# A two-layer hybrid decoder step on one core: the first output rows put into other tile places, two groups of side work recorded later, and new estimates for small matmuls

## The chip, the cores and the metric

One core of one Trainium2 chip runs one program. The metric is device time in microseconds (us), the median of the runs; lower is better. The kernel before has three runs: 3142.32, 3144.25 and 3147.87 us.

## The reference, cut to what matters

The program is one inference step of a decoder trunk of two layers over 2064 prompt tokens (16 learned ones ahead of 2048) and 8 samples of one token each. All inputs are 32-bit floats.

```
u = x @ w_in                                  # 1024 -> 5128 channels
A: 512 ch: causal conv, RG-LRU: r, i = sigmoid(xb @ w_a + b_a), sigmoid(xb @ w_x + b_x)
   log_a = -8 r softplus(-lam);  h = scan(exp(log_a), sqrt(1 - exp(2 log_a)) * i * x);  y = h * silu(z)
B: 4 heads of 128: rotary retention in chunks of 64, group norm, * silu(z)
C: 4 heads of 128: conv on q, k, v; gated delta rule in chunks of 64 (triangular solve), rms norm, * silu(z)
mix = concat(y_A, y_B, y_C)                   # 1536 channels
y = layernorm(alpha * x + mix @ w_out) * ln_w + ln_b
```

Beside y the step returns the new states of A, B and C and the last inputs of the convs, for the prompt and for the samples.

## The kernel before

**How the work is tiled.** A layer (`layer`, L551) goes through its tokens in two halves (`sblock`, L594; 1040 tokens, then 1024 with the 8 samples behind them). A half has 16 stages, listed in `STAGES` (L29): K (the keys of a delta head), A (128 channels of the RG-LRU), B (a retention head), C (a delta head). A stage projects its slabs of 128 output channels: 24 matmuls for each slab and block of tokens, since each 32-bit operand is split into a high and a low part and three products are formed over eight slabs of k. The work that follows a projection (gates, scan, retention, delta rule) is a generator that the `Pump` (L282) advances between the matmuls of the next stage's projection. The second half ends with the stages C3, B3, A3. What a branch gives is multiplied by its gate and stored to DRAM by `put_mix` (L660), on POOL's queue (`mix_d<-g`).

**The output stage** (from L1460) takes rows of 128 tokens, 17 of them. For a row, `o_load` (L1476) fetches the mixed channels (`ma`, 8 slabs; `mb`, 4 slabs) and the residual `xr`; `o_split` (L1499) casts them to high parts `ah`, `bh` on ACT and subtracts to low parts `al`, `bh[:, 1]` on DVE; then 2 x 36 matmuls of 512 columns run over the slabs of the output weights in `WO_ORDER` (L1632). Row 0's load is recorded with the last slab of A3 (`last_slab`, L1426), and the load of row r + 1 when row r starts. The output weights come in by `wo_load` (L1634): 12 slabs, each cast on ACT and subtracted on DVE or POOL; ten of them go into the `arena` as the projection has done with a part of the tokens (`wo_free`, L1664). Beside rows 0 and 1 run the ends of B3 and A3: `rglru_gates` (L1362: matmuls `pgt`, activations `r` and `ix`), `rglru_scan` (L1389), the norm of B3 (`pno`, `sn`) and the samples' retention (`samples_ret`, L1178: it loads a state `sv` on POOL's queue and makes `ps` from `swork` and `sv`).

**What sets the order.** All instructions are recorded first (`Recorder`, L62 to L259; its helper is the only line, L268, that the trace shows, so that the rows are told apart by their tiles). `cost` (L160) estimates each duration, and `order` (L190) schedules greedily: the operation that can start earliest, and of those the one recorded first. `places` (L84) adds the waits for tile places: a tag with `bufs` places is handed out in turn, and a new tile in a place waits for the last use of the old one.

**Tile places of the first rows.** Tag "g" has two places, held by B3's and A3's gates while the output stage begins. Row 0's `ah` is the next tile of that tag and takes B3's place; row 1's `ah` takes A3's, which is free when A3's `put_mix` has stored it. `bh` goes by row to "t21" (even) and "cc" (odd), row 0's `xr` to "ap", all other `xr` to "kT".

**The two other pieces.** At the start of a layer DVE computes `hba` (half the gates' biases) and `sp4` (from `softplus`, L411), which only `rglru_gates` and `rglru_scan` read, and POOL's queue copies the older two inputs of the samples' conv from one DRAM tensor to another (`out_cs<-in_convb`, 128 KB).

Of the kernel before, what the change touches and what calls it, by code (L numbers as in the profile page):

```python
# [8 lines left out]
F32 = mybir.dt.float32  # L9
F32R = mybir.dt.float32r  # L10
BF = mybir.dt.bfloat16
AF = mybir.ActivationFunctionType
OP = mybir.AluOpType
# [28 lines left out]
_V = {}  # L42
# [7 lines left out]

class Op:

    __slots__ = ("eng", "name", "emit", "cost", "succ", "left", "ready", "nbytes", "func", "port", "first", "frees", "start", "end")

    def __init__(self, eng, name, emit):
        self.eng, self.name, self.emit = eng, name, emit
        self.succ, self.left, self.ready, self.nbytes, self.func, self.port, self.first, self.frees = [], 0, 0.0, 0, None, False, 1, []


class Recorder:  # L60
# [4 lines left out]


    SETS = {"Exp": 0, "Tanh": 0, "Sqrt": 1}
    SLACK = {"PE": 0.2, "DVE": 0.07, "ACT": 0.07, "POOL": 0.1, "SP": 0.05}

    def __init__(self, tc):  # L70
# [89 lines left out]
    def cost(self, op, out, ins, kw):  # L160
        n, eng = out.free_size(), op.eng
        if eng == "PE":
            m = ins[0].free_size()
            if op.name == "transpose":
                return 0.107 * max(m, out.free_size()) / 128 + 0.002
            if ins[0].dtype == F32:
                return 2 * (max(n, m, 24) / 1200 + 0.004)
            return max(n, 64) / 2400 + 0.0135
        if op.name == "dma_start":
            op.nbytes = out.nbytes() if callable(out.nbytes) else out.nbytes  # L170
            return 0.06 if eng == "SP" else 0.55
        n = max([n] + [x.free_size() for x in ins if x.free_size() <= 2048])
        if eng == "ACT":
            return 0.165 + 0.00083 * n + 0.09 * (len(ins) > 1) + 0.19 * ("accum_out" in kw)
        if eng == "POOL":
            op.port = op.name == "tensor_tensor"
            return 0.1 + n * {"tensor_tensor": 0.00225, "memset": 0.00083}.get(op.name, 0.0011)
        near = [x for x in ins if "PSUM" not in str(x.space)]
        op.port = (sum(x.free_size() >= 8 for x in near) > 1
                   or op.name in ("tensor_scalar", "tensor_copy") and "PSUM" not in str(out.space) and bool(near))  # L180
        if op.name == "tensor_tensor_scan":
            return 0.22 + 0.00208 * n
        step = max((abs(x.ap[-1][0]) for x in ins if len(x.ap) > 1), default=1)
        return 0.15 + 0.00104 * n * (2 if step > 1 else 1) + 0.05 * (len(ins) > 2)
# [5 lines left out]
    def order(self):  # L190
        t = dict.fromkeys(("PE", "DVE", "ACT", "POOL", "SP"), 0.0)
        wait = {e: [] for e in t}
        here = {e: [] for e in t}
        pool, dma, func, out = 0.0, 0.0, None, []
        for i, op in enumerate(self.ops):
            if not op.left:
                heapq.heappush(wait[op.eng], (0.0, i))
        while True:
            best = None
            for e in t:  # L200
                w, h = wait[e], here[e]
                while w and w[0][0] <= t[e]:
                    self.move(w, h)
                s = t[e] if h else w[0][0] if w else None
                if s is not None and (best is None or s < best[0]):
                    best = s, e
            if best is None:
                break
            start, e = best
            t[e] = max(t[e], start)  # L210
            while wait[e] and wait[e][0][0] <= t[e]:
                self.move(wait[e], here[e])
            i = heapq.heappop(here[e])[1]
            op = self.ops[i]
            cost = op.cost
            if e == "DVE" and op.port and pool > start:
                cost += pool - start
            if op.func is not None and op.func != func:
                func, cost = op.func, cost + 1.28
            t[e] = end = start + cost  # L220
            if op.name == "dma_start":
                dma = max(dma, start + 0.3) + op.nbytes / 3.0e5
                end = max(dma, start + 1.6) + 0.3
            elif e == "PE":
                end += 0.2
            elif op.port and e == "POOL":
                pool = end
            op.start, op.end = start, t[e]
            out.append(i)
            done = [(j, end, e if op.name != "dma_start" else None) for j in op.succ]  # L230
            while done:
                j, at, by = done.pop()
                q = self.ops[j]
                if q.eng is not None:
                    at = t[e] if by == q.eng else at + self.SLACK[q.eng]
                q.ready = max(q.ready, at)
                q.left -= 1
                if not q.left:
                    if q.eng is None:
                        done += [(k, q.ready, None) for k in q.succ]  # L240
                    else:
                        heapq.heappush(wait[q.eng], (q.ready, j))
        assert len(out) == sum(op.eng is not None for op in self.ops)
        return out
# [94 lines left out]
def hymba_step(ctx: ExitStack, tc: tile.TileContext, x0t, x0, win, wab, wout, wg, vec, fbc, const, rope,  # L339
# [211 lines left out]
    def layer(l):  # L551
# [4 lines left out]
        def VV(name):  # L556
            a, b = _V[name]
            return vt[:, a:b]
# [3 lines left out]
        cb = lay.tile([128, 16, 3, NS], F32, name="cb", tag="cb")  # L562
        SP.dma_start(cb, convb[l])
        cs = lay.tile([128, 16, NS], F32, name="cs", tag="cs")
        G.dma_start(o_cs[l, :, :, 0:2, :], convb[l, :, :, 1:3, :])
        h0 = lay.tile([128, 4, NS], F32, name="h0", tag="h0")
        SP.dma_start(h0, rgh0[l])

        hba = lay.tile([128, 8], F32, name="hba", tag="hba")
        V.tensor_scalar(hba, vt[:, _V["ba"][0]:_V["bx"][1]], 0.5, None, op0=OP.mult)  # L570
        gcw = lay.tile([128, 48], F32, name="gcw", tag="gcw")
        V.tensor_scalar(gcw, VV("gcw"), 0.5, None, op0=OP.mult)
        sp4 = lay.tile([128, 2, 4], F32, name="sp4", tag="sp4")
        V.tensor_scalar(sp4[:, 0], VV("lam"), -1.0, None, op0=OP.mult)
        softplus(sp4[:, 1], sp4[:, 0], 128, 4, "sp")
        V.tensor_scalar(sp4[:, 0], sp4[:, 1], -4.0, None, op0=OP.mult)
        V.tensor_scalar(sp4[:, 1], sp4[:, 1], 4.0, None, op0=OP.mult)
        nea = lay.tile([128, 4], F32, name="nea", tag="nea")
        A.activation(nea, fb[:, 0:4], AF.Exp)
        V.tensor_scalar(nea, nea, -1.0, None, op0=OP.mult)  # L580
# [3 lines left out]
        SP.dma_start(rab, wab[l])  # L584
        A.copy(wabt[:, :, 0:8], rab)
        V.tensor_tensor(wabt[:, :, 8:16], rab, wabt[:, :, 0:8].bitcast(F32), op=OP.subtract)

        G.memset(carry, 0.0)
        G.memset(hcar, 0.0)
# [4 lines left out]
        def sblock(sb):  # L594
# [843 lines left out]
            for i_st, st in enumerate(STAGES[sb]):  # L1438
# [14 lines left out]
                if st == "K0":  # L1453
                    hook["pre"] = None
                    gates_c()
                    ap = wk.tile([128, 8, 4, 64], F32, tag="ap", name="ap", bufs=1)
                    tt = wk.tile([128, 32, 32], F32, tag="tt", name="tt", bufs=1)
                    t21 = wk.tile([128, 32, 32], F32, tag="t21", name="t21", bufs=1)
                    apt = None
                    if samp:  # L1460
                        apt = sm.tile([32, 16, 32], F32, tag="apt", name="apt", bufs=1)
                        G.memset(apt, 0.0)
# [8 lines left out]
        if l == DEPTH - 1:  # L1471
            rows = [(NM + r, n) for r, n in rows]
# [3 lines left out]
        def o_load(ri):  # L1476
# [7 lines left out]
            for i in range(3):  # L1484
                c0, c1 = max(r0, mix_c[i]), min(r0 + R, mix_c[i + 1])
                if c0 < c1:
                    mv_ = mix_d[i].rearrange("k p c -> p k c")[:, :, c0 - mix_c[i]:c1 - mix_c[i]]
                    SP.dma_start(ma[:, :, c0 - r0:c1 - r0], mv_[:, 0:8])
                    SP.dma_start(mb[:, :, c0 - r0:c1 - r0], mv_[:, 8:12])
            xr = big("kT", "xr", n=1024) if ri else wk.tile([128, 1024], F32, tag="ap", name="xr", bufs=1)  # L1490
            if l == 0:
                SP.dma_start(xr[:R], x0[r0:r0 + R, :])
            else:
                for i in range(r0 // 128, (r0 + R - 1) // 128 + 1):
                    c0, c1 = max(r0, 128 * i), min(r0 + R, 128 * i + 128)
                    SP.dma_start(xr[c0 - r0:c1 - r0], x1_d[i][c0 - 128 * i:c1 - 128 * i])
            return ma, mb, xr

        def o_split(ri, ma, mb, xr):  # L1499
            r0, R = rows[ri]  # L1500
            M = R if R == 128 else 32
            ah = wk.tile([128, 8, 128], F32R, tag="g", name="ah", bufs=2)
            al = wk.tile([128, 8, 128], F32R, tag="raw" if ri % 2 and ri < 14 else "tt", name="al", bufs=1)
            bh = wk.tile([128, 2, 4, 128], F32R, tag=("t21", "cc")[ri % 2], name="bh", bufs=1)
            if R == 128:
                pair = (ah, al, ma), (bh[:, 0], bh[:, 1], mb)
            else:
# [23 lines left out]
        for ri, (r0, R) in enumerate(rows):  # L1531
# [9 lines left out]
            if ri == 0:  # L1541
                cur_t = nxt["o"]
                cur_p = o_split(0, *cur_t)
            xr = cur_t[2]
            al, parts = cur_p
            if not last:
                nxt_t = o_load(ri + 1)
            ps2 = [pj(), p1(("po", "pd")[ri % 2])]
            if R < 128:
                for d in range(2):  # L1550
# [36 lines left out]
            if ri == 1:  # L1587
# [3 lines left out]
                SP.dma_start(o_hs[l], h0)  # L1591
                SP.dma_start(o_cp[l], carry)
                SP.dma_start(o_cs[l, :, :, 2, :], cs)
                pump.begin(11 * 72)
                swork = wk.tile([128, 512], F32, tag="gm2", name="swork", bufs=1)
                pump.add(samples["delta"](swork), 22)
# [195 lines left out]
```

## Time and profile before

| what | value |
|---|---|
| median of the runs | 3144.25 us |
| the profiled execution, its own time | 3149.36 us |
| its span | 3147.5 us |
| mean granted TensorE clock | 0.991 |
| PE busy | 3099.6 us, 98% |
| DVE busy | 2047.3 us, 65% |
| ACT busy | 1292.3 us, 41% |
| POOL busy | 674.0 us, 21% |
| DMA, mean | 84 GB/s |

The busy times are for the whole span. PE is TensorE's matmuls, DVE is VectorE, ACT is ScalarE, POOL is GpSimd. A granted clock of 1.00 is 2.4 GHz and one of 0.50 is 1.2 GHz. An engine's wait is listed with the instruction that waited and the one that released it.

### The profile page before, as it was taken

How to read it: one execution, taken by the hardware profiler on the slowest of the kernel's cores; microseconds unless marked ns; L12 is line 12 of the kernel's file. 1: busy time of each engine (PE TensorE's matmuls, PEld its weight loads, DVE VectorE, ACT ScalarE, POOL GpSimd, SP SyncE). 2: the span in 40 equal slices, each digit the busy share in tenths (PEclk: the TensorE clock that was granted, in tenths of full speed). 3: DMA queues.
4: the chain of work that ended last, by engine and by line, in shares of the span. 5: the costliest groups of instructions: out<-in, count | busy, mean ns of one | idle time of the engine just before them, and what ended most of it. 6: DMA issues, size and time to landing. Idle time of an engine off the chain costs nothing. (4 is left out here: it accounts for less than half of the span.)

```text
span 3147.5 us, 47379 instructions
## 1 busy us (share of the span) xinstructions
PE 3099.6 (98%) x18876; PEld 2722.0 (86%) x18876; DVE 2047.3 (65%) x3736; ACT 1292.3 (41%) x2732; POOL 674.0 (21%) x651
## 2 busy tenths in 40 slices
PE   8999999999999999999999999999999999999999
PEld 6888888899999999788778888888999999987886
DVE  6886565678666565656469865655787655656554
ACT  4455444543454454211144544445334544542100
POOL 2222132221223231111022222222222222311110
PEclk9999999999999999999999999999999999999999
DMA  4121111321111113655321212112211111136541
GB/s 156 63 69 48 56 50 58 112 79 50 49 54 52 50 60 100 193 160 163 104 104 61 71 42 68 51 58 98 85 44 49 54 59 52 51 111 184 173 140 61
DMA packets 137060, 262.96 MB, mean 84 GB/s; under 512 B 24368, under 2 KB 79600, under 8 KB 136840
## 3 DMA queue, kind: packets, MB, share of 16 engines
q1 hardware_dynamic: 113640, 179.91, 18.3%
q0 software_dynamic: 23200, 80.04, 7.0%
q8 instruction: 148, 2.42, 0.3%
q14 instruction: 72, 0.59, 0.1%
HBM read 195.13 MB, written 65.04 MB: 83 GB/s over the span
## 5 line engine op out<-in xcount | busy, mean ns | idle before, releaser
L268 PE MATMUL pj<-arena 128*128 128x512 f32 (+3 forms) x9760 | 2107.6, 360 | 11.9 <-ACT arena L268 7.6
L268 PEld LDWEIGHTS pj<-arena 128*128 128x128 f32 (+1 forms) x9760 | 1629.4, 188 | 165.9 <-ACT arena L268 7.8
L268 POOL TENSOR_TENSOR arena<-raw,arena 128x1024 fp32r<-128x1024 f32 x159 | 400.3, 2518 | 1040.3 <-ACT arena L268 1015.0
L268 ACT CAST arena<-raw 128x1024 fp32r<-128x1024 f32 x180 | 188.8, 1049 | 294.4 <-PE pj L268 176.3
L268 DVE SCALAR_TENSOR_TENSOR stg<-stg,eg,pd 128x128 f32<-128x128 f32 x264 | 91.3, 346 | 136.1 <-PE pd L268 134.6
L268 PE MATMUL pj<-arena,ah 128*128 128x512 f32 x512 | 165.6, 403 | 4.4 <-ACT ah L268 4.4
L268 ACT COPY ur<-pj 128x512 f32<-128x512 f32 (+2 forms) x160 | 80.3, 502 | 166.1 <-PE pj L268 165.7
L268 ACT ACT_TABLE_LOAD x106 | 136.0, 1283 | 4.5 <-DVE vT L268 1.9
L268 PEld LDWEIGHTS pj<-arena,ah 128*128 128x128 f32 x512 | 97.7, 191 | 27.5 <-ACT ah L268 4.7
L268 ACT COPY sw<-pj 64x512 f32<-64x512 f32 (+2 forms) x160 | 79.9, 499 | 87.0 <-PE pj L268 55.4
L268 PE MATMUL pj<-arena,al 128*128 128x512 f32 (+1 forms) x296 | 111.8, 398 | 0.3
L268 ACT ACTIVATE g<-pj 128x512 f32<-128x512 f32 (+2 forms) x120 | 61.7, 514 | 122.5 <-PE pj L268 121.6
L268 PE MATMUL pd<-kv 128*128 128x128 f32 x512 | 99.7, 276 | 0.5 <-DVE kv L268 0.5
L268 DVE SCALAR_TENSOR_TENSOR g<-g,pj 128x512 f32<-128x512 f32 (+2 forms) x120 | 69.4, 578 | 45.3 <-ACT g L268 44.9
L268 PEld LDWEIGHTS pz<-stg,wq 128*128 128x128 f32 x512 | 90.3, 189 | 9.6
L268 PE MATMUL pz<-stg,wq 128*128 128x128 f32 x512 | 98.3, 274 | 0.0
L268 ACT ACTIVATE wq<-pz,eg 64x128 f32<-64x128 f32 x128 | 43.6, 360 | 132.4 <-DVE kv L268 79.8
L268 ACT CAST bh<-mb 128x512 fp32r<-128x512 f32 x32 | 19.8, 619 | 189.3 <-PE po L268 107.6
L268 DVE SCALAR_TENSOR_TENSOR qT<-ur,gcw,qT 128x1024 f32<-128x1024 f32 (+1 forms) x48 | 78.3, 1631 | 27.8 <-ACT qT L268 27.5
L268 PEld LDWEIGHTS pd<-kv 128*128 128x128 f32 x512 | 86.6, 190 | 10.2 <-issue 1.3
L268 PE MATMUL po<-arena,ah 128*128 128x512 f32 x288 | 93.3, 401 | 0.0
L268 DVE TENSOR_TENSOR kv<-kv,pz 128x128 f32<-128x128 f32 (+1 forms) x128 | 37.0, 289 | 78.8 <-PE pz L268 78.4
(388 smaller groups left out, 5106.4 us busy)
## 6 DMA issues: line engine op xcount, KB each, us to landing
raw<-in_win SPq DMA_DIRECT2D x160, 512.0 KB, 3.3
ma<-mix_d SPq DMA_DIRECT2D x31, 512.0 KB, 5.3
mix_d<-g POOLq DMA_DIRECT2D x24, 520.0 KB, 3.5
mix_d<-g POOLq DMA_DIRECT2D x24, 512.0 KB, 3.0
raw<-in_wout SPq DMA_DIRECT2D x24, 512.0 KB, 3.3
xr<-in_x SPq DMA_DIRECT2D x16, 512.0 KB, 5.1
x_d<-yo POOLq DMA_DIRECT2D x16, 512.0 KB, 3.9
sv<-row_d POOLq DMA_DIRECT2D x16, 512.0 KB, 5.0
```

Source lines behind the costliest of these rows:

```text
L268: return lambda *args, **kw: self._r.note(self._n, op, lambda: f(*args, **kw), args, kw)
```

## The change

**Places of the first rows.** Row 0's `ah` goes to "cc", row 1's `bh` to "ap", and row 0's `xr` to "kT". The load of `xr` is a function of its own, `o_rest`; for row 0 it is recorded when row 0 starts, for the others behind `o_load`. Row 1's `ah` is thereby the first new tile of tag "g" and takes B3's gate's place, row 2's takes A3's.

```diff
-            xr = big("kT", "xr", n=1024) if ri else wk.tile([128, 1024], F32, tag="ap", name="xr", bufs=1)
+            return ma, mb
+
+        def o_rest(ri):
+            r0, R = rows[ri]
+            xr = big("kT", "xr", n=1024)
...
-            return ma, mb, xr
-
-        def o_split(ri, ma, mb, xr):
+            return xr
+
+        def o_split(ri, ma, mb):
...
-            ah = wk.tile([128, 8, 128], F32R, tag="g", name="ah", bufs=2)
+            ah = (wk.tile([128, 8, 128], F32R, tag="g", name="ah", bufs=2) if ri else
+                  wk.tile([128, 8, 128], F32R, tag="cc", name="ah", bufs=1))
...
-            bh = wk.tile([128, 2, 4, 128], F32R, tag=("t21", "cc")[ri % 2], name="bh", bufs=1)
+            if ri == 1:
+                bh = wk.tile([128, 2, 4, 128], F32R, tag="ap", name="bh", bufs=1)
+            else:
+                bh = wk.tile([128, 2, 4, 128], F32R, tag=("t21", "cc")[ri % 2], name="bh", bufs=1)
...
-            xr = cur_t[2]
+                xr = o_rest(0)
+            else:
+                xr = nxt_x
...
-                nxt_t = o_load(ri + 1)
+                nxt_t, nxt_x = o_load(ri + 1), o_rest(ri + 1)
```

**Side work.** `hba` and `sp4` are computed in a function that is recorded behind the stage K0 of the first half. The copy `out_cs<-in_convb` is recorded behind row 1 of the output stage.

```diff
-        G.dma_start(o_cs[l, :, :, 0:2, :], convb[l, :, :, 1:3, :])
...
-        V.tensor_scalar(hba, vt[:, _V["ba"][0]:_V["bx"][1]], 0.5, None, op0=OP.mult)
...
+        def recurrence_operands():
+            V.tensor_scalar(hba, vt[:, _V["ba"][0]:_V["bx"][1]], 0.5, None, op0=OP.mult)
+            V.tensor_scalar(sp4[:, 0], VV("lam"), -1.0, None, op0=OP.mult)
+            softplus(sp4[:, 1], sp4[:, 0], 128, 4, "sp")
...
                     gates_c()
+                    if sb == 0:
+                        recurrence_operands()
...
                 SP.dma_start(o_cs[l, :, :, 2, :], cs)
+                G.dma_start(o_cs[l, :, :, 0:2, :], convb[l, :, :, 1:3, :])
```

**Estimates.** A matmul's mode is the class (32, 64 or 128) of its rows and columns of the array; each change of mode is counted with 0.15 us in the order's estimate. Three forms of small 32-bit matmul are estimated at a half or a quarter of before, and an ACT instruction with an accumulated output 0.18 us cheaper.

```diff
+    SIDE = {(128, 64, 64): 2, (32, 32, 32): 2, (128, 32, 128): 4}
...
+            op.mode = tuple(32 if x <= 32 else 64 if x <= 64 else 128 for x in (k, m))
             if ins[0].dtype == F32:
-                return 2 * (max(n, m, 24) / 1200 + 0.004)
+                return 2 * (max(n, m, 24) / 1200 + 0.004) / self.SIDE.get((k, m, n), 1)
...
-            return 0.165 + 0.00083 * n + 0.09 * (len(ins) > 1) + 0.19 * ("accum_out" in kw)
+            return 0.165 + 0.00083 * n + 0.09 * (len(ins) > 1) + 0.01 * ("accum_out" in kw)
...
+            if op.mode is not None and op.mode != mode:
+                mode, cost = op.mode, cost + 0.15
```

**How the order moves: PE.** In PE's order before, at the output stage of the first layer (`pj_1682`, `pd_1683` are row 1; `pj_1696`, `po_1697` row 2; `ah_1669` is row 1's high part, `ah_1684` row 2's; `ps1`, `ps2` are the samples' retention):

```order
L268 MATMUL pd_1683<-wh_1619,bh_1671 128x512
L268 MATMUL ps1_1698<-swork_1687,ct_95 128x32
L268 MATMUL ps1_1703<-swork_1687,ct_95 128x32
L268 MATMUL ps2_1705<-scol_788,sv_1699 128x1 x7
L268 MATMUL pj_1696<-wh_1608,bh_1686 128x512
```

```order
L268 MATMUL po_1697<-wl_1620,bh_1686 128x512
L268 MATMUL po_1697<-wh_1619,bh_1686 128x512
L268 MATMUL po_1697<-arena_99,ah_1684 128x512 x2
L268 MATMUL ps2_1705<-scol_788,sv_1699 128x1
L268 MATMUL psr_1717<-ct_95,scol_788 8x128
L268 MATMUL pj_1682<-arena_99,ah_1669 128x512 x2
```

And in PE's order of the change, at the same place (`pj_1665`, `po_1666` and `ah_1658` are row 0):

```order
L273 MATMUL po_1666<-arena_99,bh_1660 128x512 x6
L273 MATMUL ps1_1698<-swork_1687,ct_95 128x32
L273 MATMUL ps1_1703<-swork_1687,ct_95 128x32
L273 MATMUL pj_1665<-arena_99,ah_1658 128x512
L273 MATMUL po_1666<-arena_99,ah_1658 128x512
L273 MATMUL ps2_1705<-scol_788,sv_1699 128x1
L273 MATMUL pj_1682<-wh_1608,bh_1671 128x512
```

Before, the samples' matmuls stood behind the first part of row 1, part of row 2 was drawn ahead of row 1's `ah` matmuls, and these came last. In the change the samples' matmuls stand inside row 0, 56 matmuls of 512 columns, 18 of the gates and 9 of B3's norm behind row 0's first; row 1 follows row 0 whole, and row 2 follows row 1.

**How the order moves: ACT.** In ACT's order before, at the gates of A3 (`r` and `ix` are the gates, `wv` their weights, `raw` an output-weight slab, `ah_1659` row 0's high part):

```order
L268 CAST wv_1645<-wgt_1624 128x2x128
L268 CAST arena_99<-raw_1646 128x1024
L268 ACTIVATE r_1641<-pgt_1647,hba_122 128x384
L268 ACTIVATE r_1641<-pgt_1648,hba_122 128x384
L268 CAST ah_1659<-ma_1625 128x1024
L268 ACTIVATE r_1641<-pgt_1650,hba_122 128x280
```

And in that of the change, where `ah_1669` is row 1's high part:

```order
L273 CAST arena_99<-raw_1650 128x1024
L273 CAST wv_1644<-wgt_1624 128x2x128
L273 ACTIVATE r_1640<-pgt_1646,hba_122 128x384
L273 ACTIVATE r_1640<-pgt_1647,hba_122 128x384
L273 CAST ah_1669<-ma_1662 128x1024
L273 ACTIVATE r_1640<-pgt_1649,hba_122 128x280
```

The slab's cast moved from behind `wv` to ahead of it, and the cast between the second and the third `r` is now row 1's; row 0's (`ah_1658`) stands in the stage B3. No instruction is added or removed on any engine; the changes of array mode on PE number 526 before and 527 in the change.

## Rows read from the trace of the kernel before

**Rows 1.** The page's busy times of the whole span.

```profile
PE 3099.6 (98%) x18876; PEld 2722.0 (86%) x18876; DVE 2047.3 (65%) x3736; ACT 1292.3 (41%) x2732; POOL 674.0 (21%) x651
```

**Rows 2.** Waits of PE, whole span: us in total, times, longest.

```profile
PE pj L268 <- ACT ah L268: 4.4, 2, 2.7
PE pgt L268 <- ACT r L268: 3.0, 2, 1.6
PE ps L268 <- DVE swork L268: 2.4, 2, 1.2
PE pno L268 <- ACT sn L268: 1.7, 2, 0.9
```

**Rows 3.** Windows: us, busy per engine (count), PEclk, DMA share, GB/s.

```profile
1190.00:1240.00 50.00, 49.75 (x345) 47.13 (x344) 22.94 (x65) 19.93 (x51) 6.07 (x7) 1.00 0.27 86
1254.73:1303.50 48.77, 41.67 (x164) 32.09 (x163) 36.86 (x56) 23.88 (x32) 7.22 (x11) 0.86 0.67 209
2820.95:2869.95 49.00, 42.95 (x177) 33.25 (x177) 37.30 (x56) 24.22 (x32) 7.09 (x10) 0.90 0.70 212
1259.10:1262.50 3.40, 3.14 (x7) 2.00 (x7) 3.02 (x5) 2.42 (x5) 0.13 (x1) 0.50 0.09 18
```

**Rows 4.** Timeline of PE, 1233 to 1299 us: start, duration, instruction, idle before.

```profile
1233.93 0.60 PE L268 MATMUL ptv<-ct,vT 128*128 128x128 f32 x4
...
1254.73 0.39 PE L268 MATMUL pj<-wh,bh 128*128 128x512 f32 x1
...
1256.12 2.26 PE L268 MATMUL pno<-ct,sn 128*128 128x128 f32 x8
...
1273.39 1.56 PE L268 MATMUL pj<-arena,bh 128*128 128x512 f32 x6
...
1298.34 0.74 PE L268 MATMUL pj<-arena,ah 128*128 128x512 f32 x2 [2.72 <-ACT ah L268]
```

**Rows 5.** Timeline of ACT, 1264 to 1299 us.

```profile
1264.41 1.05 ACT L268 CAST arena<-raw 128x1024 fp32r<-128x1024 f32 x1 [1.90 <-DMA raw<-in_wout]
1265.36 1.04 ACT L268 ACTIVATE r<-pgt,hba 128x384 f32<-128x384 f32 x2
1266.30 1.04 ACT L268 CAST ah<-ma 128x1024 fp32r<-128x1024 f32 x1
...
1297.24 1.04 ACT L268 CAST ah<-ma 128x1024 fp32r<-128x1024 f32 x1 [4.57 <-DMA mix_d<-g]
```

**Rows 6.** Timeline of POOL, 1262 to 1293 us.

```profile
1262.37 0.55 POOL L268 DMA_DIRECT2D mix_d<-g  x1 [9.59 <-PE po L268]
...
1272.49 0.57 POOL L268 DMA_DIRECT2D sv<-in_sret  x1 [8.78 <-DVE ix L268]
1275.20 1.92 POOL L268 TENSOR_TENSOR y<-r 128x1048 f32<-128x1048 f32 x1 [2.14 <-ACT r L268]
1291.11 1.08 POOL L268 DMA_DIRECT2D mix_d<-g  x2 [0.45 <-DVE g L268]
```

**Rows 7.** Timeline of DVE, 1275 to 1283 us.

```profile
1275.65 2.03 DVE L268 TENSOR_TENSOR bh<-mb,bh 128x512 fp32r<-128x512 f32 x1 [0.45 <-ACT bh L268]
...
1281.68 0.69 DVE L268 TENSOR_TENSOR bh<-mb,bh 128x512 fp32r<-128x512 f32 x1 [1.71 <-ACT bh L268]
```

**Rows 8.** DMA issues, whole span: count, KB each, us to landing.

```profile
sv<-in_sret POOLq DMA_DIRECT2D x8, 512.0 KB, 4.8
out_cs<-in_convb POOLq DMA_DIRECT2D x2, 128.0 KB, 8.0
```

**Rows 9.** Timeline of the start, POOL and PE.

```profile
2.13 1.19 POOL L268 DMA_DIRECT2D out_cs<-in_convb  x1
24.61 12.81 PE L268 MATMUL pj<-arena 128*128 128x512 f32 x43 [2.76 <-DVE arena L268]
```

**Rows 10.** Timeline of PE, 49 us: a change of array mode.

```profile
49.32 0.40 PE L268 MATMUL pj<-arena 128*128 128x512 f32 x1
49.65 0.33 PE L268 MATMUL pk<-kT 128*64 128x64 f32 x2
```

More of the change, by code (lines that the diff above doesn't have):

```diff
@@ L51 @@
 class Op:
-    __slots__ = ("eng", "name", "emit", "cost", "succ", "left", "ready", "nbytes", "func", "port", "first", "frees", "start", "end")
+    __slots__ = ("eng", "name", "emit", "cost", "succ", "left", "ready", "nbytes", "func", "port", "first", "frees", "start", "end", "mode")
     def __init__(self, eng, name, emit):
         self.eng, self.name, self.emit = eng, name, emit
-        self.succ, self.left, self.ready, self.nbytes, self.func, self.port, self.first, self.frees = [], 0, 0.0, 0, None, False, 1, []
+        self.succ, self.left, self.ready, self.nbytes, self.func, self.port, self.first, self.frees, self.mode = [], 0, 0.0, 0, None, False, 1, [], None
 class Recorder:
     SETS = {"Exp": 0, "Tanh": 0, "Sqrt": 1}
+    SIDE = {(128, 64, 64): 2, (32, 32, 32): 2, (128, 32, 128): 4}
     SLACK = {"PE": 0.2, "DVE": 0.07, "ACT": 0.07, "POOL": 0.1, "SP": 0.05}
@@ L162, in cost @@
         if eng == "PE":
-            m = ins[0].free_size()
+            m, k = ins[0].free_size(), ins[0].ap[0][1]
             if op.name == "transpose":
                 return 0.107 * max(m, out.free_size()) / 128 + 0.002
+            op.mode = tuple(32 if x <= 32 else 64 if x <= 64 else 128 for x in (k, m))
             if ins[0].dtype == F32:
-                return 2 * (max(n, m, 24) / 1200 + 0.004)
+                return 2 * (max(n, m, 24) / 1200 + 0.004) / self.SIDE.get((k, m, n), 1)
             return max(n, 64) / 2400 + 0.0135
@@ L193, in order @@
         here = {e: [] for e in t}
-        pool, dma, func, out = 0.0, 0.0, None, []
+        pool, dma, func, mode, out = 0.0, 0.0, None, (128, 128), []
         for i, op in enumerate(self.ops):
@@ L573, in layer @@
         sp4 = lay.tile([128, 2, 4], F32, name="sp4", tag="sp4")
[L574 to L577, printed above, removed]
         nea = lay.tile([128, 4], F32, name="nea", tag="nea")
@@ L586, in layer @@
         V.tensor_tensor(wabt[:, :, 8:16], rab, wabt[:, :, 0:8].bitcast(F32), op=OP.subtract)
+        def recurrence_operands():
+            V.tensor_scalar(hba, vt[:, _V["ba"][0]:_V["bx"][1]], 0.5, None, op0=OP.mult)
+            V.tensor_scalar(sp4[:, 0], VV("lam"), -1.0, None, op0=OP.mult)
+            softplus(sp4[:, 1], sp4[:, 0], 128, 4, "sp")
+            V.tensor_scalar(sp4[:, 0], sp4[:, 1], -4.0, None, op0=OP.mult)
+            V.tensor_scalar(sp4[:, 1], sp4[:, 1], 4.0, None, op0=OP.mult)
         G.memset(carry, 0.0)
```

## The prediction, made before the changed kernel ran

> **What bounds the kernel now.** The busy times come first: PE is busy 98% of the span, DVE 65% [rows 1], so that an edit gains only where PE stands still or runs slowly. The list of PE's waits tells where it stands. Four of them, two of each, once a layer, lie where the output stage begins: for row 1's `ah` 4.4 us, for the gates' `r` 3.0, for `swork` 2.4, for B3's `sn` 1.7 [rows 2]. The windows say what that is worth: a stretch of 50 us in B3 has PE busy for 49.75, while the first 49 us of the two output stages have 41.67 and 42.95, at mean granted clocks of 0.86 and 0.90 [rows 3]. A clock of 0.86 is a share of the time at 1.2 GHz in place of 2.4: one such stretch of 3.40 us is shown, and 14% of 48.77 and 10% of 49.00 us are 6.8 and 4.9 us lost, 11.7 in all, which is seven stretches of 3.4 us at a loss of 1.7 each [rows 3]. In the timelines the chain is seen: row 1's `ah` matmul starts at 1298.34 behind an idle 2.72 [rows 4]; its cast on ACT starts at 1297.24 and was released by a gate's store [rows 5], which POOL issued at 1291.11 [rows 6]. That is A3's gate, whose place row 1's `ah` needs.
>
> **The change part by part.** The sum is made against the profiled execution, 3149.4 us, 5.1 above the median.
>
> *Places.* Row 1's `ah` now takes the place of B3's gate, whose store is issued at 1262.37 [rows 6], 35 us ahead of the cast it held up, and rows 1 and 2 follow row 0 in their own order. The wait for `ah` goes: −4.4. The samples' matmuls move into row 0, away from the place where `swork` was late: −2.4. Together −6.8 [rows 2]. Row 0's cast and subtracts move into B3, where ACT is busy 19.93 and DVE 22.94 of 50 us [rows 3]: nothing, while they have that cover; without it the cast's 1.04 [rows 5] a layer. Its `xr` is loaded later, and is wanted only by the sum behind row 0's last matmul: nothing.
>
> *The gates.* Before, ACT had a slab's cast of 1.05 from 1264.41, ahead of the first `r` [rows 5], and PE waited up to 1.6 for `r` [rows 2]. In the new order this cast stands ahead of `wv`. I take 1.0 a layer, −2.0; the bounds are 0 and the whole wait, −3.0. Between the second and third `r` a cast of `ah` stands now as before, so that none is saved there.
>
> *B3's norm.* Eight transposes took 2.26 [rows 4]. Four dense ones take 0.60, of which the last shows 0.28 (its share without overlap), so 0.11 each, 0.9 for eight. They are now drawn one by one between row 0's matmuls, and 1.4 a layer could be saved. What paced them may be the product that feeds them, and then most stays: −1.0 a layer, −2.0; bounds 0 and −2.7.
>
> *The samples' state.* The first matmul that reads `sv` is reached earlier now. Its load was issued at 1272.49 [rows 6] and takes 4.8 [rows 8]: it is there at 1277.3, 22.6 us behind row 0's first matmul at 1254.73 [rows 4]. In the new order 56 matmuls of 512 columns stand ahead of it, at (1.56 − 0.39)/5 = 0.23 each [rows 4] 13.1 us; 18 of the gates, mostly of 384 columns, by their columns 2.9; nine transposes 1.0; in all 17.0. With what may be left in one layer of the waits for `r` (half of 1.5, 0.8) and `sn` (0.9) [rows 2] and one slow stretch (1.7) PE is there after 20.4, and would wait 2.2. But the load's issue waits for the gates, and these come about 1.0 earlier by the term above: +1.2, rounded to +1.0 a layer, +2.0. Bounds 0 and 2 × 2.2 = 4.4. Queued behind it on PE is row 0's rest.
>
> *The clock.* The slow stretches followed the waits [rows 2, 3]. With the idle time mostly gone I take four of seven as gone: 4 × 1.7 = −6.8. Bounds 0 and −11.7.
>
> *The start.* Both copies of a layer's `out_cs` were issued in the first 6 us, the first at 2.13, 128 KB each, 8.0 us to landing [rows 8, 9]; PE's last wait there ends at 24.61 and is 2.76 long [rows 9]. The first weights share the DMA engines with them: −0.5, by 256 KB beside the many MB that are then under way; bounds −2.8 and, where the copies now stand between two loads of slabs in the stages B3 and A3, +2. `hba` and `sp4` keep nearly their places in DVE's order: nothing, under the same cover.
>
> *Estimates.* They alter no instruction. The number of mode changes goes from 526 to 527, and one costs 0.33 − 0.23 = 0.10 (from one start to the next) [rows 10]: +0.1. What they do through the order is a rival below.
>
> *DVE beside POOL.* The subtract of `bh` took 2.03 where POOL multiplied `y` for 1.92, and 0.69 otherwise [rows 6, 7]. Moved into B3, row 0's two subtracts may meet POOL's slabs: 1.34 each, 5.4 for both layers, on DVE. PE does not wait there, so the term is nothing, and 5.4 is its price if DVE held up PE. The Trainium skill, "SBUF — State Buffer", section "Who interferes with whom", has it that a VectorE instruction with two SBUF inputs shares a port with GpSimd's reads, and that the one which comes second is blocked for the whole of the other. The row agrees with the sign, not the size of it: 1.34 of 1.92. By the rule the sum would be 4 × 1.92 = 7.7 worse if PE had no cover, and the same if it has.
>
> Sum: −6.8 − 2.0 − 2.0 + 2.0 − 6.8 − 0.5 + 0.1 = −16.0, which makes 3133.4 of the profiled 3149.4. As that execution is above the median, part of its slow stretches may not be in the others; for the median I count half of the clock's term: −12.6, **3132** from 3144.25.
>
> **The rivals.** *New waits in the old ones' place.* The wait for `sv` at its upper bound, 4.4, with a slow stretch of 1.7 behind each, 3.4, and none of the old stretches gone: −6.8 − 2.0 − 2.0 + 4.4 + 3.4 = −3.0, 3141. The same comes out if row 1's cast is late: it stands ahead of the third `r` on ACT, and needs B3's gate stored; before, row 0's cast at that place in the order began at 1266.30 [rows 5], under 4 us behind the store's issue [rows 6]. For it: 22.6 against 20.4. Against it: the chain of the gates gets shorter too.
>
> *The estimates turn the order (slower).* The scheduler draws small matmuls that it now holds to be two to four times cheaper ahead of, or behind, projections in 64 stages, and a stage's last generator then ends late. A new wait of that kind is priced by `sn`'s 0.9 [rows 2] with a slow stretch of 1.7 behind it: 2.6. Five of them undo −12.6, eight make it slower by over 6.3, nine give 3144.25 − 12.6 + 23.4 = 3155. Against it: PE is dense in mid-stage [rows 3], so slack is there to take up a shift.
>
> *More goes than I take.* All seven slow stretches vanish: −6.8 − 2.0 − 2.0 + 2.0 − 11.7 − 0.5 + 0.1 = −20.9, 3123.
>
> *The change does not do what it says*: row 1 waits all the same. The order shows row 1's cast between two of the gates' activations, long before A3's gate is stored, so that I count it within the first rival.
>
> **How the numbers follow.** My forecast has 0.58, more than that 0.12, new waits 0.20, turned order 0.10. The low end is all terms at their best, −6.8 − 3.0 − 2.7 − 11.7 − 2.8 = −27.0, 3117; the high end takes in the first rival with the copies' +2 and a little more, 3146. The rival of the order lies outside, with 0.10. A measurement of this kernel can tell about 0.2%, 6.3 us, from no change: faster is below 3138, slower above 3150.5. Faster: 0.58 + 0.12 = 0.70; same 0.20; slower 0.10.
>
> **What would show it.** Right: no wait for `ah` among PE's, row 1's first `ah` matmul within 30 us of row 0's first rather than 44, mean clocks over 0.93 in the two windows, and the wait for `swork` gone. Wrong: a wait of over 1 us for `sv` with a slow stretch behind it, `ah` waiting on a gate's store, a wait for `r` of 1.6 as before, or PE's busy share falling in stages far from the output.

## The result, and the profile after

| | before | changed |
|---|---|---|
| median | 3147.94 us (6 runs) | 3129.06 us (6 runs) |
| lowest to highest | 3142.32 to 3156.80 | 3125.47 to 3134.19 |
| ratio | | 0.9949, 95% interval 0.9936 to 0.9962 |
| profiled execution | 3149.36 | 3134.19, its span 3132.2 |

The changed kernel is faster by 0.5%; the quotient of the two medians in the table is 0.9940, inside the interval of the ratio on record. Its profiled execution is the slowest of its six, so what follows tells of a changed kernel at its worst. The page's first line and its busy times, as [rows 1]:

```profile
span 3132.2 us, 47396 instructions
PE 3089.2 (99%) x18876; PEld 2707.9 (86%) x18876; DVE 2038.0 (65%) x3736; ACT 1294.2 (41%) x2732; POOL 678.5 (22%) x651
```

PE's idle time is the span less its busy time: 47.9 us before, 43.0 now. Of the four waits of [rows 2] two are gone from the list of PE's waits (for `ah` and for `swork`), and others stand there:

```profile
PE pj L273 <- ACT arena L273: 8.9, 3, 6.8
PE ps L273 <- DMA sv<-in_sret: 4.3, 1, 4.3
PE pj L273 <- DVE arena L273: 3.4, 3, 2.7
PE pj L273 <- DVE g L273: 3.0, 4, 0.7
PE pd L273 <- DVE kv L273: 2.6, 6, 0.5
PE pno L273 <- ACT sn L273: 1.6, 1, 1.6
...
PE pgt L273 <- ACT r L273: 1.0, 2, 0.5
```

The wait for `sv` is new and stands in layer 0 alone. The next fence has windows of the changed kernel (us, busy time and count of PE, PEld, DVE, ACT, POOL, granted clock, DMA share, GB/s): the starts of the two output stages, as [rows 3], the stretch behind the wait for `sv`, and a stretch of layer 0's second half in which the delta rule's triangular blocks are inverted (called the inverses below).

```profile
1251.64:1300.41 48.77, 41.03 (x174) 32.38 (x173) 34.43 (x51) 22.99 (x31) 5.09 (x7) 0.90 0.61 188
2818.91:2867.91 49.00, 47.26 (x221) 38.12 (x220) 38.60 (x58) 23.41 (x33) 6.10 (x8) 1.00 0.73 222
1277.10:1287.20 10.10, 8.91 (x28) 7.69 (x29) 7.68 (x7) 3.41 (x3) 0.00 (x0) 0.50 0.62 190
778.00:813.00 35.00, 35.00 (x444) 33.80 (x443) 27.23 (x38) 17.05 (x33) 8.88 (x9) 1.00 0.17 55
```

The last of them answers to this window of the kernel before, where the same inverses are computed:

```profile
780.00:815.00 35.00, 33.56 (x398) 31.38 (x397) 21.00 (x22) 11.86 (x27) 7.57 (x7) 0.80 0.13 40
```

The loss of a window is its idle time and the part of it that the clock takes (its length times one less the granted clock). Layer 0's output stage lost 7.1 + 6.8 = 13.9 us before and loses 7.7 + 4.9 = 12.6 now; layer 1's lost 6.05 + 4.9 = 10.95 and loses 1.7 + 0. The inverses lost 1.4 + 7.0 = 8.4 and lose nothing; most of the 7.0 turns out below to belong to that execution. Three timelines (start, duration, instruction, idle before) add the start and the new wait. PE:

```profile
22.66 12.51 PE L273 MATMUL pj<-arena 128*128 128x512 f32 x43 [2.74 <-DVE arena L273]
...
1278.29 0.56 PE L273 MATMUL ps<-scol,sv 128*128 128x1 f32 x2 [4.33 <-DMA sv<-in_sret]
```

POOL and ACT:

```profile
1269.75 0.58 POOL L273 DMA_DIRECT2D sv<-in_sret  x1 [9.60 <-DVE ix L273]
...
1291.08 1.14 POOL L273 DMA_DIRECT2D mix_d<-g  x2 [1.85 <-DVE g L273]
```

```profile
1261.91 1.05 ACT L273 CAST ah<-ma 128x1024 fp32r<-128x1024 f32 x1 [0.17 <-issue]
...
1296.26 1.05 ACT L273 CAST ah<-ma 128x1024 fp32r<-128x1024 f32 x1 [3.61 <-DMA mix_d<-g]
```

PE's last wait of the start ends 1.95 us earlier than in [rows 9]. Row 1's cast runs at 1261.91; what now waits for A3's store (1291.08) is row 2's, at 1296.26. The spans differ by 15.3 us: 1.95 at the start, 8.4 at the inverses, 1.3 and 9.2 at the output stages make 20.9. The other 5.6 went the other way, and the experiments look for them: PE's busy time, less half of what of it lies in the stretches at 0.50, is the matmul work at full clock. The trace's clock records put 49.3 us of busy time into such stretches before and 17.5 now, so the work is 3099.6 - 24.6 = 3075.0 and 3089.2 - 8.8 = 3080.4, 5.4 more.

### The profile page after: what moved, and what is told of

Same layout as the page of the kernel before. It is cut to its first block, busy times and chain, and to the rows that moved or that the text cites. A ratio compares the mean times of both kernels' runs of the same rounds, so it can differ in the third digit from the quotient of the medians.

```text
span 3132.2 us, 47396 instructions
## 1 busy us (share of the span) xinstructions
PE 3089.2 (99%) x18876; PEld 2707.9 (86%) x18876; DVE 2038.0 (65%) x3736; ACT 1294.2 (41%) x2732; POOL 678.5 (22%) x651
## 5 line engine op out<-in xcount | busy, mean ns | idle before, releaser
L273 ACT ACT_TABLE_LOAD x106 | 136.0, 1283 | 4.5 <-DVE vT L273 1.9
L273 DVE SCALAR_TENSOR_TENSOR g<-g,pj 128x512 f32<-128x512 f32 (+2 forms) x120 | 69.5, 579 | 39.5 <-ACT g L273 38.5
L273 DVE SCALAR_TENSOR_TENSOR kT<-ur,gcw,kT 128x1024 f32<-128x1024 f32 (+1 forms) x48 | 74.0, 1541 | 19.2 <-ACT kT L273 18.7
```

Of the source, the lines that this page charges most:

```text
L273: return lambda *args, **kw: self._r.note(self._n, op, lambda: f(*args, **kw), args, kw)
```

## The experiments

Medians and ratios are to the kernel before on the same chip (3145.28, 3146.46 and 3145.51 us in the three groups of four). "Work" is PE's work at full clock in the profiled execution, worked out as above. With all three estimates it is 3080.4 to 3083.3, without them or with one of them 3074.6 to 3077.3.

| kernel | median us | ratio, 95% interval | work us |
|---|---|---|---|
| places alone | 3128.34 | 0.9943, 0.9931 to 0.9956 | 3074.8 |
| estimates alone | 3143.12 | 0.9992, 0.9983 to 1.0001 | 3082.3 |
| side work alone | 3144.42 | 0.9996, 0.9987 to 1.0005 | 3077.3 |
| changed, `sv` estimated late | 3140.13 | 0.9986, 0.9977 to 0.9995 | 3083.2 |
| changed, `sv` loaded early | 3132.47 | 0.9958, 0.9945 to 0.9971 | 3083.3 |
| changed, row 1's wait put back | 3145.91 | 0.9996, 0.9985 to 1.0008 | 3082.2 |
| changed, rows 0 and 1 changed about | 3131.89 | 0.9956, 0.9944 to 0.9967 | 3082.1 |
| places, side work, `sv` early: the fastest | 3122.97 | 0.9929, 0.9917 to 0.9941 | 3074.6 |
| places, side work | 3130.99 | 0.9950, 0.9934 to 0.9966 | 3075.3 |
| the fastest with the mode estimate | 3128.94 | 0.9945, 0.9931 to 0.9959 | 3075.6 |
| the fastest with the small matmuls' estimate | 3128.58 | 0.9942, 0.9929 to 0.9955 | 3074.7 |
| the fastest with ACT's estimate | 3125.95 | 0.9936, 0.9924 to 0.9948 | 3077.1 |

**Places alone.** Of the change's diff only the blocks on `o_load`, `o_rest`, `o_split` and the rows' loop:

```diff
+            ah = (wk.tile([128, 8, 128], F32R, tag="g", name="ah", bufs=2) if ri else
+                  wk.tile([128, 8, 128], F32R, tag="cc", name="ah", bufs=1))
```

> The kernel before with the tile places of the first rows alone (row 0's high part, row 1's low slabs, the residual's load). Theory A (the places carry what the output stages gain, the estimates what the inverses gain, the copies what the start gains): 4 to 8 us faster than before (ratio 0.997 to 0.999); PE no longer waits for ah and swork in either layer, a wait for sv of 2 to 4 us stands in layer 0, the slow clock stretch at about 798 us (13.65 us long before) is still there, and the start is as before. Theory B (the three parts only work together, since the order is set anew by each): under 2 us, with waits of 1 us and more left where the output stages begin. Theory C (the places carry nearly all of it, and the slow stretch at 798 is a matter of the execution): 14 us and more faster (0.9955 or less), with no slow stretch at 798.

It has the whole gain: 0.9943. Theory A named the right part and less than half of its size; theory C has the size, but it wanted no slow stretch at the inverses, and one of 3.4 us stands there. The windows at its output stages:

```profile
1250.10:1298.90 48.80, 45.82 (x199) 36.49 (x198) 37.68 (x56) 24.07 (x32) 6.12 (x9) 0.93 0.67 205
2809.50:2858.50 49.00, 44.98 (x203) 35.36 (x202) 38.04 (x57) 23.94 (x32) 6.02 (x8) 0.97 0.70 218
```

They lose 3.0 + 3.4 and 4.0 + 1.5, together 11.9 against 24.9 before: 13.0 us of gain, more than the changed kernel has there. Its list of waits has 1.8 for `sv` in layer 0, and 1.8 for `ah` in layer 1, which is row 2's:

```profile
PE pg L268 <- DVE tn L268: 2.6, 2, 1.3
PE ps L268 <- DMA sv<-in_sret: 1.8, 1, 1.8
PE pj L268 <- ACT ah L268: 1.8, 1, 1.8
```

The slow stretch at the inverses is there with 3.4 us and not 13.65, behind the same wait for `tn` as before, 1.3 us. So at least 5.1 of the 7.0 us that the clock took in the profile of before belong to that execution.

**Estimates alone.** Of the diff only `cost`, `order` and `SIDE`.

```diff
+                return 2 * (max(n, m, 24) / 1200 + 0.004) / self.SIDE.get((k, m, n), 1)
...
+                mode, cost = op.mode, cost + 0.15
```

> The kernel before with the changed estimates alone. Theory A: 6 to 9 us faster (ratio 0.997 to 0.998), by the slow stretch at the inverses of the second half of layer 0 (13.65 us at half clock, 6.8 lost) and the waits of 1.3 us for tn in front of them; the wait for ah (4.4) is still there. Theory C (the slow stretch at 798 comes and goes by itself): no change (0.999 to 1.001), with the stretch in the profile. My prediction's own term for the estimates was nothing but +0.1, with a loss as the rival: slower by up to 11 us, waits at stage ends.

No change that can be told: 0.9992. The stretch at the inverses and the wait for `tn` are gone, as theory A had it, but the time is theory C's. PE's work went from 3075.0 to 3082.3.

**Side work alone.**

```diff
-        G.dma_start(o_cs[l, :, :, 0:2, :], convb[l, :, :, 1:3, :])
...
+                    if sb == 0:
+                        recurrence_operands()
```

> The kernel before with the two pieces of side work moved alone (the copy of the conv inputs behind row 1, hba and sp4 behind K0). Theory A: 1 to 2.5 us faster (0.9992 to 0.9997, hardly to be told from none by time), all of it in the first 60 us: the 400th wide matmul 1.5 to 2 us earlier in the trace. Theory B: none at the start, since the estimates reorder the start as well. The prediction's term was -0.5 (bounds -2.8 and +2).

By time it is no different. Its last wait of the start ends at 23.65, that of the kernel with the places alone, which still has the two copies there, at 26.07:

```profile
23.65 11.49 PE L268 MATMUL pj<-arena 128*128 128x512 f32 x43 [2.72 <-DVE arena L268]
```

```profile
26.07 11.77 PE L268 MATMUL pj<-arena 128*128 128x512 f32 x43 [3.35 <-DVE arena L268]
```

With 24.61 before and 22.66 in the changed kernel, the side work, copies and small operands together, costs the start 1 to 3 us in these executions.

**The wait for `sv`: a late estimate.** Three lines in `Op`, `cost` and `order`, of which the core is:

```diff
+            op.late = 4.0 if out.tensor.name.startswith("sv") else 0.3
...
-                end = max(dma, start + 1.6) + 0.3
+                end = max(dma, start + 1.6) + op.late
```

> The changed kernel with one estimate more: the landing of the samples' states sv is estimated 3.7 us later, and by that the order draws the first matmuls on sv not into row 0 but behind row 2. It tells what the new wait costs. Theory A: the wait of 4.3 us for sv in layer 0 and the three slow stretches behind it (10.2 us at half clock, 5.1 lost) go, 5 to 9 us faster than the changed kernel (0.992 of before or less). Rival D (the stretch has another cause, or the wait turns into one for the last slabs or the next row): as fast as the changed kernel within 2 us, 0.9945 to 0.9955 of before.

Both theories fail: it is 11 us slower than the changed kernel. The first read of `sv` moved behind row 2 as wanted, but the waits went to later states, 5.4 us in two:

```profile
2978.06 2.64 PE L274 MATMUL ps<-scol,sv 128*128 128x1 f32 x16 [3.69 <-DMA sv<-in_sret]
```

An estimate for one kind of load sets the whole order anew, so this run does not tell what the wait cost.

**The wait for `sv`: an early load.** A3's conv output fills half of its place; the first state goes into the other half.

```diff
-                c = big("tab", "c", bufs=1) if end else big("kT", "c")
+                if end:
+                    cz = wk.tile([128, 2, 1048], F32, tag="tab", name="c", bufs=1)
+                    samples["cz"] = cz
+                    c = cz[:, 0]
+                else:
+                    c = big("kT", "c")
...
+                    if h == 0:
+                        vb, ss = (samples["cz"][:, e, :1024].rearrange("p (b c) -> p b c", b=NS) for e in range(2))
```

> The changed kernel with the first state of the samples' retention loaded into the unused half of the place that holds A3's conv output, so that its load waits for the rope tables' last use and no longer for A3's gates; the order of PE is that of the changed kernel word for word. Theory A (the new wait of 4.3 us for sv in layer 0 cost itself and the slow clock stretch of 10.2 us behind it): the wait for sv and the stretch at 1277 us are gone, 5 to 9 us faster than the changed kernel, 0.992 to 0.9935 of before. Rival (the wait moves on to the next late thing, row 1's casts or a slab, or the stretch stays without the wait): under 2 us faster, 0.9943 to 0.995.

The wait for `sv` and the slow stretch behind it are gone, and nothing is gained: 0.9958. The rival holds by the time. Row 2's cast now waits for A3's store. In layer 0 that costs PE 1.0 us, with the low part `al` behind it; the larger wait is in layer 1, where the changed kernel had no wait for `sv` (POOL, ACT, PE):

```profile
2850.26 1.13 POOL L273 DMA_DIRECT2D mix_d<-g  x2 [17.54 <-DVE g L273]
```

```profile
2857.30 2.00 ACT L273 CAST ah<-ma 128x1024 fp32r<-128x1024 f32 x2 [5.47 <-DMA mix_d<-g]
```

```profile
2858.40 0.73 PE L273 MATMUL pj<-arena,ah 128*128 128x512 f32 x2 [2.62 <-ACT ah L273]
```

PE does not come to it sooner there: it is ready for row 2 at 2858.40 - 2.62, 43.4 us behind row 0's first matmul (2812.35), as in the changed kernel (2862.35 and 2818.91). A3's store comes later, 37.9 us behind that matmul and not 34.7. The edit left PE's order as it was but for ten places, and it changed ACT's: a later row's cast of `bh` moved ahead of A3's activation `s`, and waits for its load. First this kernel, then the changed one:

```profile
2840.22 0.62 ACT L273 CAST bh<-mb 128x512 fp32r<-128x512 f32 x1 [5.56 <-DMA mb<-mix_d]
...
2842.16 1.08 ACT L273 ACTIVATE s<-s 128x1048 f32<-128x1048 f32 x1
```

```profile
2844.37 1.08 ACT L273 ACTIVATE s<-s 128x1048 f32<-128x1048 f32 x1 [1.21 <-DVE s L273]
2845.36 0.62 ACT L273 CAST bh<-mb 128x512 fp32r<-128x512 f32 x1
```

From row 0's first matmul `s` is 29.8 us away and was 25.5. So this run does not tell the price of the wait for `sv` by itself.

**Row 1's wait put back.**

```diff
+            if ri == 1:
+                wk.tile([128, 8, 128], F32R, tag="g", name="ah", bufs=2)
```

> The changed kernel with one unused tile of tag g taken ahead of row 1's high part, so that row 1 waits again for A3's gate's place, as in the kernel before; everything else of the change stays. Theory A (row 1's place is the part that pays, by the wait and the slow stretches behind it): waits for ah of 2 to 5 us are back, slow stretches are back, 8 to 16 us slower than the changed kernel, 0.9975 to 1.000 of before. Rival (row 0's early split in the place cc pays): within 4 us of the changed kernel, 0.9937 to 0.996.

The whole gain is gone: 0.9996. So row 1's place is what pays, and row 0's early split without it is worth nothing. Here too the order is set anew; that the loss is not that of any new order is seen from the next run, which keeps row 1 free of the wait and keeps the gain. The wait shows elsewhere than expected. As row 2 is drawn ahead of row 1 again, row 1's casts are not what PE meets first: row 2's next product needs the PSUM place of row 0, which DVE's sum `yy` empties behind A3's scan.

```profile
PE pj L273 <- DVE yy L273: 6.7, 2, 3.3
```

```profile
1288.10 0.79 PE L273 MATMUL pj<-wh,bh 128*128 128x512 f32 x1 [3.33 <-DVE yy L273]
```

That it is row 2's product is read from the order, the trace shows only its tiles' names. The two waits of 3.3 are not the whole loss: this profiled execution (3140.58) is 5 us below its median and that of the changed kernel 5 us above its own.

**Rows 0 and 1 changed about.**

```diff
-            ah = (wk.tile([128, 8, 128], F32R, tag="g", name="ah", bufs=2) if ri else
+            ah = (wk.tile([128, 8, 128], F32R, tag="g", name="ah", bufs=2) if ri != 1 else
```

> The changed kernel with rows 0 and 1 changed about: row 1's high part in the place cc, row 0's in B3's gate's place, as before the change; row 1 has no wait for a gate, and row 0 is split as late as in the kernel before. Theory A (row 1's place pays): no wait for ah of over 1 us, as fast as the changed kernel within 4 us, 0.993 to 0.996. Rival (row 0's early split pays): most of the gain is lost, 0.998 and more, with idle PE at the start of row 0. The order draws the samples' first state behind row 2 here, as in the run with the late estimate for sv, which was 11 us slower than the changed kernel: if that is what counts, it is 0.998 and more too, with the waits for sv far behind row 0.

0.9956, the changed kernel's gain within the intervals: theory A. Its price for row 0's late split is in the gates:

```profile
PE pgt L273 <- ACT r L273: 4.2, 2, 2.1
...
PE pgt L273 <- ACT wv L273: 2.6, 2, 1.3
```

Here too the samples' states are read behind row 2, and no wait for `sv` is in the list, so that this place in the order is not by itself what made the run with the late estimate slow.

**Without the estimates.** Places, side work and the early load; `cost` and `order` as before.

```diff
-            if op.mode is not None and op.mode != mode:
-                mode, cost = op.mode, cost + 0.15
```

> Places, side work and the early load of sv, with the estimates of the kernel before. If the estimates are worth the 2 us that they showed alone, it is 1 to 3 us slower than the run with the early load and all of the change; if they cost where the output stage of layer 0 begins (7.7 us of idle PE in the changed kernel against 3.0 with the places alone), it is 2 to 5 us faster, 0.991 of before or less.

The estimates cost here, 9.5 us by the medians where I had 2 to 5. The fastest of all: 3122.97, 0.9929, below each of the others' medians, and its slowest run (3125.86) is faster than the fastest with the estimates and the early load (3131.03). Both were profiled at a mean clock of 0.998. First it, then the one with the estimates:

```profile
span 3118.9 us, 47371 instructions
...
PE 3079.4 (99%) x18876; PEld 2707.5 (87%) x18876; DVE 2047.5 (66%) x3736; ACT 1291.9 (41%) x2732; POOL 677.7 (22%) x651
```

```profile
span 3130.7 us, 47393 instructions
...
PE 3088.4 (99%) x18876; PEld 2705.8 (86%) x18876; DVE 2039.7 (65%) x3736; ACT 1293.1 (41%) x2732; POOL 677.7 (22%) x651
```

The same 18876 matmuls keep PE busy for 9.0 us longer, and the idle time is 42.3 against 39.5.

**The early load, without the estimates.** As the kernel above, `sv` loaded as in the change:

```diff
-                    c = cz[:, 0]
+                c = big("tab", "c", bufs=1) if end else big("kT", "c")
```

> Places and side work of the change, estimates of before, the samples' first state loaded where the change loads it. With the early load the same kernel took 3123.0 us, 0.9929. Theory A (the early load pays once the estimates are out): 3 to 6 us slower than that, 0.994 to 0.995, with a wait for sv of 2 us and more. Rival (the early load pays nothing here either, since row 2's high part then waits for A3's gate): within 2 us of it, 0.9923 to 0.9935.

3130.99, 8 us slower (6.6 by the ratios), but with runs from 3122.99 to 3136.92, whose mean clocks go from 0.998 to 0.992. The profiled one is the fastest of them, has a wait of 1.6 for `sv`, under the 2 that theory A wanted, and lies 2.3 us above the profiled one with the early load. Theory A by the medians; the size is not settled, as the intervals overlap. This kernel is also the change without its estimates, and its 0.9950 is the change's 0.9949: there the estimates cost nothing that shows.

**One estimate at a time**, on the fastest kernel.

```diff
+            if op.mode is not None and op.mode != mode:
+                mode, cost = op.mode, cost + 0.15
```

> The kernel with places, side work and early load (3123.0 us; PE busy 3079.4 in its profile) with one estimate of the change added: 0.15 for a change of array mode. In its order the projection's matmuls are cut into 1615 runs rather than 1589. Theory E (the estimates cost PE time by cutting the projection into more runs, about 0.3 us a run by the 9 us and 30 runs that all three estimates showed): 6 to 9 us slower, 0.995 to 0.996, PE busy 3085 to 3088 at the same clock. Rival F (what the estimates cost are waits, not PE time): PE busy within 2 us of 3079.4, and the loss, if any, is in the list of waits.

```diff
+                return 2 * (max(n, m, 24) / 1200 + 0.004) / self.SIDE.get((k, m, n), 1)
```

> The same kernel with the other estimate added, three forms of small matmul at a half or a quarter. 1612 runs rather than 1589. Theory E: 5 to 8 us slower, 0.9945 to 0.9955, PE busy 3084 to 3087. Rival F: PE busy within 2 us of 3079.4.

```diff
-            return 0.165 + 0.00083 * n + 0.09 * (len(ins) > 1) + 0.19 * ("accum_out" in kw)
+            return 0.165 + 0.00083 * n + 0.09 * (len(ins) > 1) + 0.01 * ("accum_out" in kw)
```

> The same kernel with the third estimate added, ACT's accumulated outputs 0.18 cheaper. 1591 runs, two more. Theory E: within 1.5 us of the kernel without it, 0.9925 to 0.9935, PE busy within 1.5 us of 3079.4; only the waits of the delta heads for ACT (qk for wq, 3.6 us in four) may change, by 3 us at most.

Medians 6.0, 5.6 and 3.0 us above the fastest kernel's (5.0, 4.1 and 2.2 by the ratios, as these ran in another group); the intervals overlap with its own, so that each loss is likely and not certain. Theory E falls: with 26 and 23 more runs of projection matmuls in the order the work is 3075.6 and 3074.7 against 3074.6, though the theory had some 5 us and more (the busy times, 3083.7 and 3083.0, hold slow stretches too, at mean clocks of 0.996). What they add is in the waits, of the first and of the second:

```profile
PE pz L271 <- DVE stg L271: 4.3, 2, 3.0
```

```profile
PE qk L269 <- ACT kv L269: 9.0, 3, 4.3
```

where the kernel without them has 2.1 for `stg` and none for `kv`. ACT's estimate, which the theory had within 1.5 us, adds no idle time (38.3 us against 39.5) but 2.5 us of work. That all three together add 8.7 us of PE time and none alone over 2.5 is measured, in one execution each; why is open.

## Why the prediction was right

The forecast was 3132 us, 0.9961 of the median it started from (3144.25); measured were 3129.06 and 0.9949. Right in sign, and the steps one by one:

- **`ah`, -4.4, and `swork`, -2.4: right.** Both waits are gone [rows 2], and putting row 1's wait back alone undid the gain. Row 1's first `ah` matmul came 27 us behind row 0's first in layer 1 (2846.14 against 2818.91), under the 30 that I set, and 38 us in layer 0 (1289.66 against 1251.64), over it, with the wait for `sv` between.
- **`r`, -2.0: right.** 3.0 before, 1.0 now.
- **B3's norm, -2.0: more.** The transposes stand singly between row 0's matmuls and none waits; only the ninth still waits for `sn`, 1.6 in layer 0:

```profile
1252.57 0.27 PE L273 MATMUL pno<-ct,sn 128*128 128x128 f32 x1
1252.60 0.48 PE L273 MATMUL pj<-wl,bh 128*128 128x512 f32 x1
1252.91 0.27 PE L273 MATMUL pno<-ct,sn 128*128 128x128 f32 x1
```

  A matmul and a transpose take 0.34 from one start to the next, 0.23 and 0.11, which is the dense price and so the upper bound of -2.7.
- **`sv`, +2.0, 1.0 a layer: mis-sized and in one layer.** 4.3 in layer 0, nothing in layer 1. PE came to it 22.3 us behind row 0's first matmul (1278.29 - 4.33 - 1251.64) and not after 20.4, but the load took 8.4 us to land in that stretch, not 4.8, with two loads of residual rows and two of slabs beside it, and it was issued 18.1 us behind that matmul (17.8 before), not 1.0 earlier. The run without the wait was no faster, as row 2's cast was late in its turn; since ACT's order moved there too, the wait's own price stays open. The step lacked "what is late next".
- **The clock, -6.8, four of seven stretches: right here.** Three of 3.4 us remain in layer 0, none in layer 1.
- **The start, -0.5: mis-sized**, 1.95, within its bounds.
- **The estimates, +0.1: the step that failed**, in what it counted. I counted changes of array mode, 526 and 527, and took the rest as a rival with 0.10. Even the price of 0.10 is not the mode's for sure: a matmul of 512 columns followed by a transpose in the same mode takes 0.31 to the next start as well (1252.60 to 1252.91 above). What they did is larger in both directions: the waits at the inverses went (1.4, beside a slow stretch that was mostly that execution's), and PE's matmul work grew by 5.4. Alone they come out even, 0.9992, and in the change as it stands too (0.9949 with them, 0.9950 without); with the early load they cost 9.5 us.
- **DVE beside POOL, nothing: right.** Row 0's two subtracts run in B3 at 1.23 and 0.69, undisturbed, since neither fell beside a POOL subtract (2.38 from 1201.57):

```profile
1195.56 1.23 DVE L273 TENSOR_TENSOR al<-ma,ah 128x1024 fp32r<-128x1024 f32 x1 [0.86 <-ACT ah L273]
...
1204.70 0.69 DVE L273 TENSOR_TENSOR bh<-mb,bh 128x512 fp32r<-128x512 f32 x1 [1.30 <-ACT bh L273]
```

  I set the loss of 1.34 against the whole of POOL's 1.92, which is a misreading: when the subtract of [rows 7] began, at 1275.65, only 1.47 of it were left. The changed kernel has the same on a slab's subtract, which otherwise takes 1.23. In layer 1 POOL had 0.60 left, and 0.46 was lost (POOL, DVE):

```profile
2837.22 1.92 POOL L273 TENSOR_TENSOR y<-r 128x1048 f32<-128x1048 f32 x1 [2.51 <-ACT r L273]
```

```profile
2838.54 1.69 DVE L273 TENSOR_TENSOR arena<-raw,arena 128x1024 fp32r<-128x1024 f32 x1
```

  In both the subtract lost what was left of POOL's multiplication, less some 0.13.

The first rival's wait for `sv` came at its upper bound (4.3 of 4.4) with slow stretches behind it, but the old stretches went all the same. The sum was right partly because errors cancelled: the stretch at the inverses, which was in no term, went with 8.4, most of it by the execution that was profiled, and 5.4 of matmul work came.

## What to carry to other kernels

Where tile places are handed out in turn, look at which work holds the place that the next tile will get: freeing one tile of such a wait was the whole gain here, and the next tile in turn then became the late one, so name what the engine will meet behind a wait before it is taken away. An order made from estimates should be judged part by part on the chip: estimates closer to measured durations gave an order that was no better, and cost 9.5 us in one pair of kernels and nothing in another.

## What was not expected of the hardware

The same wait of 1.3 us at the inverses was followed by 13.65 us at half clock in the profiled execution of before, by 3.4 us in those of the kernels with the places alone and the side work alone, and by none in the fastest kernel. In the execution of before itself the same wait in layer 1 had none behind it, as the wait and its window show:

```profile
2368.32 1.20 PE L268 MATMUL pg<-tn,ap 32*32 32x32 f32 x64 [1.30 <-DVE tn L268]
```

```profile
2361.00:2380.00 19.00, 17.12 (x321) 15.64 (x321) 13.04 (x12) 6.62 (x17) 4.56 (x5) 1.00 0.10 29
```

The wait alone sets neither whether a slow stretch comes nor its length, and a price for it read from one execution can be off by the whole 6.8 us.

The order of the same 18876 matmuls changes their busy time by 9.0 us at the same mean clock (3088.4 against 3079.4) with 527 and 528 changes of array mode; it does not go with the number of runs into which the projection is cut, as two kernels with 1612 and 1615 runs in their orders show at most 1.0 us more work than that with 1589.
